# Output projection of a hybrid attention layer: six of eight pairs as three couples of seven block products each, with operands made beside attention and kept in DRAM

## The chip, the cores and the metric

The kernel runs on 1 core of one Trainium2 chip. The metric is the device time of one execution in microseconds (us). Before the change it is 680.48 us, the median of 3 runs (680.47 to 680.68).

The engines go by these names: PE multiplies matrices (PEld is its weight load), DVE, ACT and POOL work element by element, SP issues most of the DMA transfers. Each engine runs its own instructions strictly in order and waits on semaphores for what others make.

## The reference

One layer over 1024 rows of 1024 columns. After an adaptive layer norm, one input projection feeds 8 forgetting-attention heads and 8 stick-breaking heads of 64 columns each; their gated outputs go through one output projection, are scaled by a gate, added to the scaled input and normalised again.

```python
u = _layer_norm(x) * (1.0 + scale[:, None, :]) + shift[:, None, :]
h = u @ w_in[layer]
fq, fk, fv, fg, ff, sq, sk, sv, sg = _split_columns(h)
...
y_fox = _from_heads(jnp.concatenate(fox_out, axis=2)) * jax.nn.silu(fg)
y_sb = _from_heads(jnp.concatenate(sb_out, axis=2)) * jax.nn.silu(sg)
y = jnp.concatenate([y_fox, y_sb], axis=-1) @ w_out[layer]
resid = DEEPNORM_ALPHA * x + gate[:, None, :] * y
x = _layer_norm(resid, ln_g[layer], ln_b[layer])
```

## The kernel before, in words

**Precision.** A matrix operand is kept as two parts: a rounded one ("hi", in the type fp32r) and the remainder ("lo"). A product of two such operands takes three matmuls, hi x hi, lo x hi and hi x lo. Making the two parts costs an engine two operations: a rounding copy and a subtraction.

**Work units.** The 16 heads are taken as 8 pairs: pairs 0 to 3 stick-breaking, 4 to 7 forgetting attention. A unit (p, h, i) is one head h of pair p and one block i of 128 query rows, 128 units in all. In a unit PE makes the scores S (L483, L484). For a stick-breaking unit ACT takes sigmoids, DVE scans (L514, L518) and POOL makes the product `be` (L520); for a forgetting unit DVE, ACT and POOL (`a`, L499) make the softmax. Two units later (LAG = 2) PE transposes the result (T, L537) and multiplies it with the values (pv, L554); POOL applies the gate path (ty, L570), and the outcome goes to DRAM (`y_dr`, L578), pair 7's to SBUF as y7h, y7l.

**Order.** PE's order is written out by hand. Between the units stand small steps of "filler": the projections of the following pairs (m for q, k and gate, L312 to L314; v, L370 to L372), rationed by FILL per pair. The other engines' order comes from a scheduler that places instructions by its own estimate of times.

**Weights.** `fetch_w` brings a piece of projection weight: a DMA into a raw tile (L123, tag "wraw", only 2 buffers), the rounding copy (L127) and the remainder (L128) on POOL, into a ring of RING = 5. An m weight is fetched as two halves (named 3_1_0, 3_1_1 for pair 3, matrix 1), a v weight, which serves two pairs, as four quarters (v1_0 to v1_3).

**Output projection before.** During pairs 4 to 6 `gen_split_out` (L890 to L899) takes 16 pieces of w_out through the same fetch, with a gate product (L125) ahead, and stores both parts in `wo_dr`. `load_y` (L910 to L918) loads gated outputs again and splits them on POOL. `o_step` (L937 to L939) is the projection itself: 8 row blocks, 2 column halves (the last block in 512, 256 and 256 columns), 8 pairs, 3 matmuls each. It runs as `tail` beside the last units and behind them; `o_half` adds the residual, normalises and stores.

## Time and profile before

The times and the profile are of the kernel before. Spans and busy times are of one profiled execution.

| what | us |
| --- | --- |
| time, median of 3 runs | 680.48 |
| span of the profiled execution, first to last instruction | 678.6 |
| what lies around the span, by the difference to the median | 1.9 |
| PE busy | 668.3 |
| DVE busy | 485.9 |
| POOL busy | 405.2 |
| ACT busy | 382.6 |

No device time of the profiled execution is given apart from its span; its own time is taken as the span with the 1.9 us around it. A row of a group of instructions reads: line, engine, operation, output and inputs with their shapes, count, then busy time in us and the mean of one in ns, then the idle time of the engine just ahead of them and what ended it. A row of a timeline reads: start, duration, engine, line, operation. A row of a DMA issue ends with the KB of one and the median time from issue to landing. Matmuls overlap, so the durations of single ones add up to more than the time that passes.

### The profile page before, as it was taken

What the parts mean: (1) busy time and instruction counts of PE and PEld (TensorE: products, weight loads), DVE (VectorE), ACT (ScalarE), POOL (GpSimd) and SP (SyncE); (2) the same over time, 40 slices, a digit from 0 to 9 for tenths busy, and PEclk for the clock granted to TensorE, in tenths of its full rate; (3) what the DMA queues carried; (4) which work ended last, traced back from release to release, by engine and by line L of the source; (5) the groups of instructions that cost most, each with busy time, mean ns of one, the idle gap of its engine ahead of it and who ended that gap; (6) DMA issues with size and microseconds to landing.
All of it is one profiled execution on the core that took longest, in us unless ns stands there. A gap on an engine that the chain in (4) does not pass through costs nothing.

```text
span 678.6 us, 11231 instructions
## 1 busy us (share of the span) xinstructions
PE 668.3 (98%) x3713; PEld 571.2 (84%) x3713; DVE 485.9 (72%) x1001; ACT 382.6 (56%) x889; POOL 405.2 (60%) x530
## 2 busy tenths in 40 slices
PE   8999999999999999999999999999999999999995
PEld 4888898888998888889988888889988888888885
DVE  6787779868677777686776675766676777775645
ACT  5576468757567667576675564655565766521000
POOL 5560279755357556556378878785785365655412
PEclk9999999999999999999999999999999999999998
DMA  9983432112101112122124555263452297153301
GB/s 326 401 312 126 139 79 75 41 28 67 29 20 56 54 42 57 40 54 56 49 93 144 151 164 174 87 201 112 127 169 59 70 350 302 59 177 107 120 32 63
DMA packets 46474, 81.55 MB, mean 120 GB/s; under 512 B 5264, under 2 KB 20176, under 8 KB 46416
## 3 DMA queue, kind: packets, MB, share of 16 engines
q1 hardware_dynamic: 44832, 76.37, 35.1%
q10 hardware_dynamic: 1584, 4.47, 2.1%
q8 instruction: 29, 0.48, 0.3%
q14 instruction: 29, 0.24, 0.1%
HBM read 60.34 MB, written 16.29 MB: 113 GB/s over the span
## 4 chain that ended last, share of the span: by engine, by line
PE 97%; DMA 1%; DVE 0%; POOL 0%; ACT 0%; issue 0%; SPq 0%; POOLq 0%
PE m L312 11%; PE m L314 10%; PE m L313 10%; PE pv L554 10%; PE T L537 9%; PE S L484 5%; PE S L483 5%; PE o L939 4%; PE o L937 4%; PE o L938 4%; PE v L370 4%; PE v L372 4%; PE v L371 4%; PE st_q L647 1%; PE st_k L647 1%; PE st_late L647 1%
## 5 line engine op out<-in xcount | busy, mean ns | idle before, releaser
L540 DVE TENSOR_TENSOR pt<-T,pt 128x512 fp32r<-128x512 f32 (+2 forms) x192 | 102.7, 553 | 43.8 <-ACT pt L539 42.2
L539 ACT CAST pt<-T 128x512 fp32r<-128x512 f32 (+2 forms) x192 | 88.9, 479 | 64.5 <-PE T L537 62.5
L312 PE MATMUL m<-uh,whi 128*128 128x512 f32 x304 | 123.3, 405 | 0.1
L314 PE MATMUL m<-uh,wlo 128*128 128x512 f32 x304 | 119.8, 394 | 0.0
L313 PE MATMUL m<-ul,whi 128*128 128x512 f32 x304 | 119.7, 394 | 0.0
L520 POOL TENSOR_TENSOR be<-be,kp 128x127 f32<-128x127 f32 (+3 forms) x64 | 78.9, 1234 | 36.2 <-DVE kp L518 24.4
L554 PE MATMUL pv<-pt,v 128*128 128x512 f32 x320 | 82.8, 388 | 0.0
L514 DVE TENSOR_TENSOR_SCAN kp<-kp,floor 128x128 f32<-128x128 f32 (+3 forms) x64 | 58.6, 915 | 17.6 <-ACT kp L506 17.4
L499 POOL TENSOR_SCALAR a<-a,l 128x1024 f32<-128x1024 f32 (+3 forms) x64 | 48.4, 756 | 34.3 <-DVE l L497 26.0
L483 PE MATMUL S<-k,q 128*128 128x512 f32 (+5 forms) x192 | 68.8, 360 | 0.0
L314 PEld LDWEIGHTS m<-uh,wlo 128*128 128x128 f32 x304 | 57.1, 188 | 13.7
L496 ACT ACTIVATE a<-a,nm 128x1024 f32<-128x1024 f32 (+3 forms) x64 | 49.8, 779 | 28.6 <-DVE nm L491 28.1
L312 PEld LDWEIGHTS m<-uh,whi 128*128 128x128 f32 x304 | 57.2, 188 | 10.2 <-PE T L537 0.3
L484 PE MATMUL S<-kl,qz 128*128 128x512 f32 (+5 forms) x192 | 65.2, 341 | 0.0
L313 PEld LDWEIGHTS m<-ul,whi 128*128 128x128 f32 x304 | 57.3, 188 | 9.0
L554 PEld LDWEIGHTS pv<-pt,v 128*128 128x128 f32 x320 | 55.5, 189 | 8.9
L570 POOL TENSOR_TENSOR ty<-ty,sg 64x256 f32<-64x256 f32 x64 | 46.9, 733 | 23.4 <-issue 12.2
L491 DVE CUSTOM_DVE_ANT_0 a<-S,fb 128x1024 f32<-128x1024 f32 (+3 forms) x64 | 48.2, 753 | 16.9 <-PE S L484 12.0
L456 ACT CAST qz<-q 64x128 fp32r<-64x128 f32 x128 | 37.3, 296 | 34.2 <-PE S L484 33.0
L506 ACT ACTIVATE kp<-S 128x384 f32<-128x384 f32 (+4 forms) x96 | 44.0, 494 | 21.5 <-PE S L484 20.2
L370 PE MATMUL v<-whi_v,uh 128*128 128x256 f32 (+1 forms) x192 | 54.7, 285 | 0.0
L372 PE MATMUL v<-wlo_v,uh 128*128 128x256 f32 (+1 forms) x192 | 54.2, 282 | 0.0
(296 smaller groups left out, 1628.3 us busy)
## 6 DMA issues: line engine op xcount, KB each, us to landing
raw<-in_w_qkg_dram SPq DMA_DIRECT2D x38, 256.0 KB, 2.7
wss<-in_w_ss_dram SPq DMA_DIRECT2D x14, 512.0 KB, 8.1
x<-in_x_dram SPq DMA_DIRECT2D x8, 512.0 KB, 7.1
k<-k SPq DMA_DIRECT2D x32, 128.0 KB, 2.3
wg<-in_w_gate_dram SPq DMA_DIRECT2D x8, 512.0 KB, 4.9
raw_o<-in_w_out_dram SPq DMA_DIRECT2D x16, 256.0 KB, 3.0
fb<-f_dr ACTq DMA_DIRECT2D x8, 512.0 KB, 4.5
wo_dr<-whi_o SPq DMA_DIRECT2D x16, 256.0 KB, 2.1
```

The source lines that it names most:

```text
L312: nc.tensor.matmul(acc, hi[:, c], u_hi[kt][:, s], start=(kt == 0), stop=False)
L313: nc.tensor.matmul(acc, hi[:, c], u_lo[kt][:, s], start=False, stop=False)
L314: nc.tensor.matmul(acc, lo[:, c], u_hi[kt][:, s], start=False, stop=(kt == NB - 1))
L370: nc.tensor.matmul(acc[:, :n], u_hi[kt][:, ts_], hi[:, s], start=(kt == 0), stop=False)
L372: nc.tensor.matmul(acc[:, :n], u_hi[kt][:, ts_], lo[:, s], start=False, stop=(kt == NB - 1))
L483: nc.tensor.matmul(S[:, s, :w], qst[p][h][:, qs], kst[p][h][:, ks], start=True, stop=False)
L484: nc.tensor.matmul(S[:, s, :w], z, klo[p][:, ks], start=False, stop=True)
L520: nc.gpsimd.tensor_tensor(be[:, :ke - 1], be[:, :ke - 1], kp[:, 1:ke], op=ALU.mult)
L537: nc.tensor.transpose(tp[:, b * P:(b + 1) * P], a[:, kb * P:(kb + 1) * P], ident)
L539: nc.scalar.copy(hi[:, :n, qo:qo + P], t3)
L540: lows[:] = [nc.vector.tensor_tensor(lo[:, :n, qo:qo + P], t3, hi.bitcast(F32)[:, :n, qo:qo + P], op=ALU.subtract)]
L554: nc.tensor.matmul(acc2[:, :, q0:], vt[p][:, kb, h * P:(h + 1) * P], pt[:, :, q0:], start=(kb == 0), stop=(kb == last))
```

## The change

The output projection of pairs 0 to 5 is taken as three couples of two pairs (NC = 3). Row blocks are taken in four pairs (ROWS), columns in two halves, so each couple is a product of 2 x 2 blocks by 2 x 2 blocks. Instead of eight block products it makes seven from sums and differences of blocks (Winograd's form of Strassen's scheme): four early ones, A11 x B11, S2 x T2, S3 x T3, S1 x T1, and three late ones, P4, P2 and P3. Pairs 6 and 7 go the direct way (`plain`).

The operands are made in 28 pieces: `weight_piece` (12), `weight_plain` (4) and `y_piece` (12). Each loads into one of the two raw tiles, may multiply by the gate, is split by an ACT copy and a POOL subtraction (`halves`), then forms four sums of 128 columns in place (`less`: on POOL during pairs 1 to 3, on DVE later), is split again and stored to DRAM. `along` steps this beside the filler from pair 1 on, one step per PACE = 3 filler steps, so that a piece holds its raw tile for some 12 to 15 of them. Before, this work on w_out lay in pairs 4 to 6 alone. In the tail the loads read ready operands (`load_early`, `load_late`, `w_block`, `w_plain`), the accumulators are summed on ACT and DVE, and the residual is added by ACT and POOL half by half.

The core of the diff; the new tail follows these products in the order early 0, early 1, direct blocks, early 2, early 3, late ones, and the last row block by itself:

```diff
-    SPACE = 10
+    PACE = 3
...
+    NC = 3
+    ROWS = ((6, 7), (4, 5), (2, 3), (0, 1))
+    EARLY = (("A11", "B11"), ("S2", "T2"), ("S3", "T3"), ("S1", "T1"))
+    LATE = {"P4": ("A22", "T4"), "P2": ("A12", "B21"), "P3": ("S4", "B22")}
...
-            nc.gpsimd.tensor_tensor(be[:, :ke - 1], be[:, :ke - 1], kp[:, 1:ke], op=ALU.mult)
+            prods[:] = [nc.gpsimd.tensor_tensor(be[:, :ke - 1], be[:, :ke - 1], kp[:, 1:ke], op=ALU.mult)]
...
-    def gen_split_out():
-        for pr in range(NPAIR):
-            for h in range(2):
-                s = slice(h * 512, h * 512 + 512)
-                with after(*scaled[BEHIND:BEHIND + 1]):
-                    hi, lo = fetch_w(f"o{pr}_{h}", w_out[pr * P:(pr + 1) * P, s], 512, gate[:, s])
-                nc.sync.dma_start(wo_dr[0, pr, :, s], hi.bitcast(F32)[:, :512])
-                nc.sync.dma_start(wo_dr[1, pr, :, s], lo.bitcast(F32)[:, :512])
-                for _ in range(SPACE):
+    def tied():
+        return after(*(scaled[BEHIND:BEHIND + 1] or prods))
+
+    def halves(raw, n, key, to):
+
+        both = ring_set(key)
+        nc.scalar.copy(both[:, 0, :n], raw[:, :n])
+        with tied():
+            nc.gpsimd.tensor_tensor(both[:, 1, :n], raw[:, :n], both.bitcast(F32)[:, 0, :n], op=ALU.subtract)
+        return both.bitcast(F32)
+
+    def less(to, a, b, op=ALU.subtract):
+        eng = nc.vector if scaled else nc.gpsimd
+        with tied():
+            eng.tensor_tensor(to, a, b, op=op)
...
+    def weight_piece(c, q):
+        raw = raw_tile(f"ow_{c}_{q}")[:, :512]
+        r4 = raw.rearrange("p (a b q) -> p a b q", a=2, b=2)
+        cols = slice(q * P, q * P + P)
+        for a in range(2):
+            pr = 2 * c + a
+            nc.sync.dma_start(r4[:, a], w_out[pr * P:(pr + 1) * P, :].rearrange("p (b c) -> p b c", b=2)[:, :, cols])
+        yield
...
+        both = halves(raw, 3 * P, f"ob_{c}_{q}", None)
+        for x in range(2):
+            nc.sync.dma_start(wo_dr[c, 0:3, :, x, cols].rearrange("o p q -> p o q"),
+                              both[:, x, :3 * P].rearrange("p (o q) -> p o q", q=P))
+        yield
+        b21, b22, b11, b12 = parts_of(raw)
+        less(b11, b12, b11)
+        less(b12, b22, b12)
+        less(b22, b22, b11)
+        less(b21, b21, b22)
+        yield
+        both = halves(raw, 4 * P, f"ot_{c}_{q}", None)
...
+            _, make, *args = pieces.pop(at[0])
+            for _ in make(*args):
+                for _ in range(PACE):
                     yield
...
+    def block(t, late, what, acc, cols=slice(0, 512), ends=(True, True)):
+
+        y, w = what
+        for c in range(NC):
+            yh, yl = (y_set[t, c, late][:, x, Y_AT[y] * P:][:, :P] for x in range(2))
+            hi, lo = (v[:, cols] for v in wo[w, c])
+            nc.tensor.matmul(acc, yh, hi, start=(ends[0] and c == 0), stop=False)
+            nc.tensor.matmul(acc, yl, hi, start=False, stop=False)
+            nc.tensor.matmul(acc, yh, lo, start=False, stop=(ends[1] and c == NC - 1))
+            yield
...
+    def along(main, side):
+        for x_ in main:
+            next(side, None)
+            yield
...
-        gen_m(2, 0), gen_m(2, 1), gen_v(1),
-        beside(chain([gen_m(2, 2), gen_m(3, 0), gen_m(3, 1), gen_m(3, 2)]), gen_forget()),
-        gen_m(4, 0), gen_m(4, 1), gen_v(2),
-        beside(chain([gen_m(4, 2), gen_m(5, 0), gen_m(5, 1), gen_m(5, 2),
-                      gen_m(6, 0), gen_m(6, 1), gen_v(3), gen_m(6, 2),
-                      gen_m(7, 0), gen_m(7, 1)]), gen_split_out()),
+        along(chain([
+            gen_m(2, 0), gen_m(2, 1), gen_v(1),
...
+            gen_m(7, 0), gen_m(7, 1)]), operands),
```

How the instructions stand now is shown at three places. First, POOL around the first quarter of weight v1, which PE first uses behind the scores of unit (1,0,7) in both kernels. In before (whi and wlo are the two parts, be and kp a unit's product, ty a gated output):

```order
L127 TENSOR_SCALAR whi_2_1_1_1743<-raw_2_1_1_1741 128x512
L128 TENSOR_TENSOR wlo_2_1_1_1744<-raw_2_1_1_1741,whi_2_1_1_1743 128x512
L521 MEMSET be_0_1_5_1456 128x1
L520 TENSOR_TENSOR be_0_1_5_1456<-be_0_1_5_1456,kp_0_1_5_1455 128x767
L127 TENSOR_SCALAR whi_v1_0_1933<-raw_v1_0_1931 128x528
L128 TENSOR_TENSOR wlo_v1_0_1934<-raw_v1_0_1931,whi_v1_0_1933 128x528
L521 MEMSET be_0_1_6_1502 128x1
L520 TENSOR_TENSOR be_0_1_6_1502<-be_0_1_6_1502,kp_0_1_6_1501 128x895
```

In the changed kernel (w is a tile with both parts, ow a raw tile of w_out):

```order
L539 TENSOR_TENSOR be_1_0_6_1898<-be_1_0_6_1898,kp_1_0_6_1897 128x895
L955 TENSOR_TENSOR ow_0_2_1868<-ow_0_2_1868,gate_88 128x512
L146 TENSOR_SCALAR w_v1_0_1961<-raw_v1_0_1959 128x528
L589 TENSOR_TENSOR ty_1_0_1_1906<-ty_1_0_1_1906,sg_1_1279 64x256
L147 TENSOR_TENSOR w_v1_0_1961<-raw_v1_0_1959,w_v1_0_1961 128x528
L540 MEMSET be_1_0_7_1950 128x1
L539 TENSOR_TENSOR be_1_0_7_1950<-be_1_0_7_1950,kp_1_0_7_1949 128x1023
L146 TENSOR_SCALAR w_v1_1_1966<-raw_v1_1_1964 128x528
L147 TENSOR_TENSOR w_v1_1_1966<-raw_v1_1_1964,w_v1_1_1966 128x528
L146 TENSOR_SCALAR w_v1_2_1971<-raw_v1_2_1969 128x528
```

The first quarter's split moved from behind the product of unit (0,1,5) to behind that of (1,0,6), nine units later, and the second quarter's from behind (1,0,1) to behind (1,0,7).

Second, POOL around weight 3_1, which PE first uses behind the scores of unit (2,0,7). In before its first half stands around the product of (1,1,7):

```order
L127 TENSOR_SCALAR whi_3_1_0_2817<-raw_3_1_0_2815 128x512
L128 TENSOR_TENSOR wlo_3_0_1_2605<-raw_3_0_1_2602,whi_3_0_1_2604 128x512
L521 MEMSET be_1_1_7_2432 128x1
L520 TENSOR_TENSOR be_1_1_7_2432<-be_1_1_7_2432,kp_1_1_7_2431 128x1023
L128 TENSOR_TENSOR wlo_3_1_0_2818<-raw_3_1_0_2815,whi_3_1_0_2817 128x512
```

In the changed kernel (oy and w_ys are a piece of gated outputs):

```order
L934 TENSOR_TENSOR w_ys_0_0_2870<-oy_0_0_2718,w_ys_0_0_2870 128x512
L589 TENSOR_TENSOR ty_2_0_1_2860<-ty_2_0_1_2860,sg_2_2508 64x256
L540 MEMSET be_2_0_7_2912 128x1
L539 TENSOR_TENSOR be_2_0_7_2912<-be_2_0_7_2912,kp_2_0_7_2911 128x1023
L146 TENSOR_SCALAR w_3_1_0_2923<-raw_3_1_0_2921 128x512
L147 TENSOR_TENSOR w_3_1_0_2923<-raw_3_1_0_2921,w_3_1_0_2923 128x512
```

It moved eight units, to behind the product of the very unit behind whose scores PE uses it.

Third, POOL around weight 4_2, which PE first uses behind the scores of unit (4,0,7). In before:

```order
L520 TENSOR_TENSOR be_3_0_7_3541<-be_3_0_7_3541,kp_3_0_7_3540 128x1023
L127 TENSOR_SCALAR whi_4_2_0_4065<-raw_4_2_0_4063 128x512
L521 MEMSET be_3_1_0_3618 128x1
L128 TENSOR_TENSOR wlo_4_2_0_4066<-raw_4_2_0_4063,whi_4_2_0_4065 128x512
L520 TENSOR_TENSOR be_3_1_0_3618<-be_3_1_0_3618,kp_3_1_0_3617 128x127
```

In the changed kernel (a is a forgetting unit's softmax):

```order
L539 TENSOR_TENSOR be_3_1_7_4230<-be_3_1_7_4230,kp_3_1_7_4229 128x1023
L955 TENSOR_TENSOR ow_2_2_4261<-ow_2_2_4261,gate_88 128x512
L934 TENSOR_TENSOR w_ot_2_1_4203<-ow_2_1_4042,w_ot_2_1_4203 128x512
L518 TENSOR_SCALAR a_4_0_7_4289<-a_4_0_7_4289,l_4_0_7_4291 128x1024
L146 TENSOR_SCALAR w_4_2_0_4276<-raw_4_2_0_4274 128x512
L147 TENSOR_TENSOR w_4_2_0_4276<-raw_4_2_0_4274,w_4_2_0_4276 128x512
```

Its two parts moved from just behind the product of (3,0,7) to behind the softmax of (4,0,7), and on SP its load now follows the stores of the piece w_ot_2_1.

## The prediction

> **What bounds the kernel now.** I read the busy shares and the chain that ended last first, then PE's own waits, then busy time by stretch.

> ```profile
> PE 668.3 (98%) x3713; PEld 571.2 (84%) x3713; DVE 485.9 (72%) x1001; ACT 382.6 (56%) x889; POOL 405.2 (60%) x530
> PE 97%; DMA 1%; DVE 0%; POOL 0%; ACT 0%; issue 0%; SPq 0%; POOLq 0%
> PE sc_all L179 <- POOL ident masks.py:199: 1.5, 1, 1.5
> PE xT_early L256 <- ACT x L222: 0.9, 1, 0.9
> PE st_q L647 <- ACT uh L270: 0.4, 1, 0.4
> ```

> PE is busy for 98% of the span, and the whole list of what it waited for is these three, 2.8 us in the first 15. So any work taken off PE shortens the kernel by its own length, and any wait put in front of PE lengthens it by its own length: nothing stands by to absorb either.

> ```profile
> 136.80:341.00 204.20, 204.20 (x1215) 179.91 (x1215) 150.28 (x261) 134.66 (x326) 117.14 (x162) 1.00 0.18 47
> 640.00:660.00 20.00, 20.00 (x87) 16.15 (x87) 9.63 (x15) 0.00 (x0) 4.60 (x6) 1.00 0.14 53
> L937 PE MATMUL o<-woh,whi_y 128*128 128x512 f32 (+1 forms) x119 | 46.1, 388 | 0.0
> L937 PE MATMUL o<-woh,y7h 128*128 128x512 f32 (+1 forms) x17 | 6.5, 382 | 0.0
> ```

> The columns of a stretch are its length, then busy time and count of PE, weight load, DVE, ACT and POOL, then the granted clock. In 640 to 660 us, inside the output projection, 87 matmuls take 20.00 us: one 512-column matmul starts every 0.23 us. The 0.388 us of the group is each one's own duration, and they overlap, so removed matmuls are priced at 0.23. POOL is at 117 of 204 us in pairs 1 to 3 (136.8 to 341.0): the change lays new work on it there.

> **What is removed.** L937 to L939 have 119 + 17 each, 408 matmuls, worth 384 of 512 columns. In the new program seven block products for four row pairs, three couples and three matmuls are 252, and pairs 6 and 7 direct are 4 x 4 x 2 x 3 = 96: 348. So 36 x 0.232 = 8.4 us less for PE, all of it on the path.

> **What is added beside attention, and where it stands.** Every operand piece costs POOL an optional gate product, two remainders and four sums of 128 columns.

> ```profile
> L125 POOL TENSOR_TENSOR raw_o<-raw_o,gate 128x512 f32<-128x512 f32 x16 | 20.7, 1294 | 6.6 <-DMA raw_o<-in_w_out_dram 6.6
> L918 POOL TENSOR_TENSOR wlo_y<-yr,whi_y 128x384 fp32r<-128x384 f32 x8 | 8.1, 1018 | 0.5
> L520 POOL TENSOR_TENSOR be<-be,kp 128x127 f32<-128x127 f32 x8 | 3.7, 464 | 0.2 <-DVE kp L514 0.2
> L127 POOL TENSOR_SCALAR whi<-raw 128x512 fp32r<-128x512 f32 x38 | 23.5, 620 | 14.1 <-PE m L313 7.6 <-DMA raw<-in_w_qkg_dram 5.0 <-DVE l L497 0.6
> L128 POOL TENSOR_TENSOR wlo<-raw,whi 128x512 fp32r<-128x512 f32 x38 | 49.2, 1297 | 1.3 <-PE v L372 0.3
> L570 POOL TENSOR_TENSOR ty<-ty,sg 64x256 f32<-64x256 f32 x64 | 46.9, 733 | 23.4 <-issue 12.2 <-DVE ty L569 8.3 <-POOL a L499 0.8
> ```

> In pairs 1 to 3 the new program has 9 gate products, 14 remainders of 384 columns, 13 of 512 and some 52 sums: 9 x 1.29 + 14 x 1.02 + 13 x 1.30 + 52 x 0.46 = 67 us, so POOL goes from 117 to 184 of 204. The work itself still fits and costs nothing where POOL is idle; what costs is its place. A piece holds one of the two raw tiles for its whole life, so the fetches of the next pair's weights are left with one, and each half must be loaded, rounded and split before the next load may begin. In the new order they have slid back with it: in before the splits stand two to ten units ahead of PE's first use in pairs 1 to 3, mostly six or more, now zero or one (two for two halves).

> What such a place is worth is read from a unit's product, behind which the split now queues, and from a fetch:

> ```profile
> 162.18 1.33 POOL L128 TENSOR_TENSOR wlo_v<-raw_v,whi_v 128x528 fp32r<-128x528 f32 x1
> 167.05 0.28 PE L370 MATMUL v<-whi_v,uh 128*128 128x264 f32 x1
> 167.79 0.28 PE L370 MATMUL v<-whi_v,uh 128*128 128x264 f32 x1
> 237.94 0.39 PE L484 MATMUL S<-kl,qz 128*128 128x512 f32 x1
> 242.36 0.28 PE L484 MATMUL S<-kl,qz 128*128 128x128 f32 x1
> 242.85 2.00 POOL L520 TENSOR_TENSOR be<-be,kp 128x1023 f32<-128x1023 f32 x1 [1.52 <-DVE kp L518]
> 244.84 0.42 POOL L520 TENSOR_TENSOR be<-be,kp 128x127 f32<-128x127 f32 x1
> raw<-in_w_qkg_dram SPq DMA_DIRECT2D x38, 256.0 KB, 2.7
> raw_v<-in_w_vf_dram SPq DMA_DIRECT2D x4, 264.0 KB, 2.7
> ```

> From the last score matmul of a row block 7 (ends 238.33) to the end of its product on POOL (244.85) are 6.5 us; of a row block 0 (242.64 to 245.26) 2.6. A fetch is 2.7 + 0.62 + 1.30 = 4.6 us, 4.7 for the 528-column quarters. One quarter of a v weight gives PE 0.74 us of work (167.05 to 167.79) on first use; a half of another weight 12 x 0.232 = 2.8. In before even the last quarter of v1 was split (163.5) before PE began the first (167.05).

> Now the sites, in the order of the program. "After S" counts from the end of the scores behind which PE meets the weight.

> - **v1.** PE meets it right behind the scores of (1,0,7). The first remainder stands behind a y product of POOL that DVE feeds, some 4.3 us after S. The second quarter's load may start only then, and its split stands behind the product of (1,0,7), 6.5 after S: another 4.1. The third is a pure chain, 4.7 less 0.7: 4.0. The fourth has a unit of PE work ahead of it: 2.6. Sum 15.
> - **3_1.** The split stands right behind the product of (2,0,7), PE's use right behind its scores: 6.5 + 0.62 = 7.1 until the rounded half is there, and the remainder 1.30, of which two matmuls cover 0.46: 8.0.
> - **4_2.** The product of (3,1,7) ends 2.7 after the scores of (4,0,7), which is where PE wants the weight (3.8 us of PE work lie between the two scores). Behind it on POOL stand a gate product (1.29) and a remainder (1.30); SP has the store of that remainder queued ahead of the load, so load, rounding and remainder follow: 2.7 + 1.29 + 1.30 + 2.7 + 0.62 = 8.6, and 0.84 for the remainder: 9.5.
> - **v2 and v3**, like v1: v2's first remainder behind the product of (3,1,0) and four POOL operations (2.6 + 0.4 + 0.7 + 0.6 + 1.3 + 1.3 = 6.9), then 2.7, 1.2 and 0.8 of chain: 11.5. v3 by the same steps 10.5.
> - **2_2.** Second half's remainder behind the product of (1,1,7), with 2.8 of PE work since its scores: 6.5 + 1.3 - 2.8 = 5.0, and some more by queued sums: 5.3.
> - **2_1, 3_0, 3_2, 4_0, 4_1.** The chain between two halves, 4.6 plus an attention product of 0.4 to 2.0, against 2.8 of work: 1.8 to 3.8 each by that, 12.7 together with their places.

> Together 15 + 8.0 + 9.5 + 11.5 + 10.5 + 5.3 + 12.7 = 72.5 us. From 5_0 on the pieces are fewer and the splits two or more units ahead, v3 aside: nothing.

> The least that no idle POOL could remove is the fetch chain itself and the two products that stand ahead: v1 9, v2 5, v3 5, 3_1 7, 4_2 8, or 34 us. The most is not bounded by these rows: a split behind a piece is also a product behind a piece, and PE's transposes come two units (8.5 us at 204.2 / 48 per unit) after scores whose product takes 6.5, so 2 us of slack meet pieces of 1.0 to 1.3 an operation. I add nothing for that and up to 15 us for the range.

> **The clock.** After its last matmul PE is idle:

> ```profile
> 671.00:678.60 7.60, 0.46 (x4) 0.26 (x3) 3.58 (x8) 0.82 (x2) 1.84 (x4) 0.66 0.18 70
> 673.00:674.00 1.00, 0.00 (x0) 0.00 (x0) 1.00 (x3) 0.37 (x1) 0.55 (x1) 0.75 0.00 0
> 674.00:675.00 1.00, 0.00 (x0) 0.00 (x0) 1.00 (x3) 0.45 (x2) 0.82 (x2) 0.50 0.00 0
> ```

> The granted clock is at half some 2 us after work ended at 671.5. About ten of my waits are longer than that. How long the half clock would last into the work behind a wait no row shows: between nothing and a whole unit of 4.25 us at half speed, 2.1 us each, so 0 to 21. I take nothing in the sum, since several of these waits are followed by another at once, and keep 21 for the range. [...]

> **The tail.** Its loads are rows of 512 KB:

> ```profile
> wol<-wo_dr SPq DMA_DIRECT2D x8, 512.0 KB, 7.8
> ```

> The last early y operand of row pair 2 is loaded into a ring tile freed shortly before PE wants it, behind 1.5 MB on the same queue: a wait of 0 to 8, I take 3, in a stretch where POOL is at 4.6 of 20. Evacuations on DVE (9.6 of 20) and the end behind the last matmul, 7.1 us, stay as they are. ACT's rounding copies lie beside its 56%.

> **The sum.** On the profiled execution: 678.6 - 8.4 + 72.5 + 3 = 745.7. The median of the runs, 680.48, is 1.9 above the span, so 747.6, call it 748. Likeliest alone 725 to 770.

> **Rivals.**

> - *Only the bare chains wait.* POOL's real pace lets the splits through earlier than queued products of 6.5 us suggest (a stalled PE makes no new scores, so POOL catches up). Then 680.5 - 8.4 + 34 = 706. Against it: the order on POOL is fixed, and the 6.5 us run from PE's own last scores.
> - *Backlog and clock.* The transposes miss their products too, and half clock follows the waits: 748 + 15 to 36, 763 to 784. For it: POOL at 184 of 204.
> - *Faster.* Early waits push PE back against POOL and SP, the later splits regain their lead, and only the saving is left, 680.5 - 8.4 = 672. It decides at the point where the split's end lies before PE's first use, so the 6.5 us from score to product would have to shrink under 2. Nothing in the rows does.
> - *It does less than it says.* The matmuls go, but a wait of the same size comes, within 0.2% (1.4 us) of before, which is about what a measurement of this kernel can tell from no change. It needs all sites but one to vanish.

> **Chances.** Forecast 0.60, bare chains 0.13, backlog and clock 0.20, faster 0.05, no change 0.01, slower by less than 700 0.01. The range reaches from just under the bare chains, 705, into the third case, 785. Slower by over 0.2% is 0.94, within 0.01, faster 0.05.

> **What would show it.** PE's waits list, three rows before, should be led by m and v matmuls waiting for POOL's splits, v1 near 15 us and the sum near 70; PE's busy time should fall by 8 us at a full clock; POOL should be near 90% in pairs 1 to 3; the granted clock should dip behind the longest waits. I am wrong if those waits are under 30 us in sum, if the longest waits are for T on POOL's products, or if the time lost lies in the tail.

## The result, and the profile after

| what | before | after |
| --- | --- | --- |
| time, median of 4 runs each, us | 680.48 (680.26 to 680.68) | 783.12 (781.92 to 784.33) |
| ratio to before, 95% interval | | 1.1509 (1.1493 to 1.1525) |
| span of the profiled execution, us | 678.6 | 780.6 |
| matmuls | 3713 | 3668 |
| PE busy, us | 668.3 | 694.7 |
| mean granted clock of PE | 0.996 | 0.949 |

The kernel became 102.6 us slower, where 67.5 was forecast: inside the range, at its upper end. The page of the changed kernel, first its busy times, then PE and its granted clock in 40 slices, then the chain that ended last:

```profile
PE 694.7 (89%) x3668; PEld 577.8 (74%) x3668; DVE 507.9 (65%) x1050; ACT 428.2 (55%) x976; POOL 467.4 (60%) x605
PE   8999999876978879886996899995999999998895
PEclk9999999995989979998897999997899999999998
PE 11%; POOL 4%; DMA 3%; DVE 3%; ACT 2%; issue 1%; SPq 0%; POOLq 0%; DVEq 0%; ACTq 0%
```

Two things are to be read from the first line. PE stands idle for 780.6 - 694.7 = 85.9 us instead of 678.6 - 668.3 = 10.3, which is 75.6 more. And PE is busy for 26.4 us longer although it has fewer matmuls: the same work went slower. The slices say where: from the eighth on, in pairs 1 to 5, PE falls again and again to between 5 and 8 tenths, and the granted clock dips in several of the same places (the 10th, 12th, 15th, 19th, 22nd and 28th slice). The chain has PE at 11% where it had 97%: it no longer runs along PE.

What PE waited for (total, times, longest); before, this list had three rows and 2.8 us:

```profile
PE v L389 <- POOL w_v L146: 19.4, 8, 4.2
PE m L331 <- POOL w L146: 19.0, 4, 8.7
PE m L333 <- POOL w L147: 8.5, 6, 3.8
PE v L391 <- POOL w_v L147: 7.2, 9, 2.0
PE m L333 <- POOL be L540: 3.7, 5, 1.2
PE T L556 <- DVE pt L559: 3.4, 4, 2.6
PE o L1058 <- DMA w_ye<-yb_dr: 3.0, 1, 3.0
PE o_P L1058 <- DMA yl_att<-yb_dr: 2.3, 1, 2.3
```

L146 is the rounding copy and L147 the remainder of a projection weight on POOL, L331 to L333 and L389 to L391 the matmuls that use them. The first four rows are 54.1 us. Three smaller rows that name the zeroing L540, which on POOL stands right ahead of the product a split is queued behind, belong to the same waits: 61.0 in all, called split waits below. The transposes T, for which the forecast feared a backlog, wait 3.4.

The stretches around the sites of the forecast (columns as before: length, busy time of PE, weight load, DVE, ACT, POOL, then granted clock, DMA share, GB/s):

```profile
136.20:406.90 270.70, 227.21 (x1234) 190.84 (x1233) 152.45 (x262) 150.74 (x355) 186.38 (x257) 0.92 0.34 96
145.00:165.00 20.00, 15.69 (x75) 12.22 (x74) 11.11 (x18) 10.83 (x25) 14.90 (x23) 1.00 0.33 93
165.00:195.00 30.00, 20.26 (x93) 16.59 (x92) 12.58 (x22) 10.93 (x25) 19.54 (x24) 0.72 0.37 93
222.00:236.00 14.00, 9.14 (x38) 6.84 (x37) 7.72 (x13) 6.37 (x14) 11.07 (x14) 0.79 0.29 85
262.00:290.00 28.00, 20.91 (x96) 16.46 (x95) 13.70 (x21) 12.93 (x30) 15.85 (x22) 0.82 0.21 64
355.00:385.00 30.00, 21.19 (x123) 18.66 (x120) 12.88 (x24) 12.40 (x31) 20.98 (x28) 0.83 0.40 112
404.00:430.00 26.00, 17.17 (x87) 14.13 (x86) 12.08 (x28) 11.40 (x23) 15.27 (x18) 0.80 0.34 103
525.00:555.00 30.00, 20.45 (x106) 17.44 (x105) 10.74 (x30) 10.22 (x26) 16.84 (x18) 0.77 0.41 121
```

Length less PE's busy time is the idle time of a site. Beside it stands what the half clock cost there, worked out from the distances between matmul starts in the stretches of half clock against those of the same shapes in before:

| site (stretch) | idle forecast, us | idle measured, us | lost to half clock, us |
| --- | --- | --- | --- |
| v1 (165 to 195) | 15 | 9.7 | 4.1 |
| 2_2 (222 to 236) | 5.3 | 4.9 | 2.0 |
| 3_1 (262 to 290) | 8.0 | 7.1 | 2.9 |
| v2 (355 to 385) | 11.5 | 8.8 | 2.6 |
| 4_2 (404 to 430) | 9.5 | 8.8 | 1.9 |
| v3 (525 to 555) | 10.5 | 9.6 | 2.8 |
| 2_1 (145 to 165), 3_0, 3_2, 4_0, 4_1 together | 12.7 | 13.0 | 0 |
| tail | 3 | 7.2 | 3.2 |
| smaller waits elsewhere | 0 | 6 | 0 |

Pairs 1 to 3 take 270.7 us where they took 206.4 (the row shown later with the last experiment). POOL is busy for 186.4 of them, 184 was forecast, but that is 69% of the longer stretch and not 90%.

One site in full, 3_1. First PE (start, duration, instruction, the wait ahead of it), then POOL:

```profile
270.70 0.40 PE L503 MATMUL S<-kl,qz 128*128 128x512 f32 x1
278.01 0.79 PE L331 MATMUL m<-uh,w 128*128 128x512 f32 x1 [6.91 <-POOL w L146]
280.38 0.63 PE L332 MATMUL m<-ul,w 128*128 128x512 f32 x1
280.81 0.63 PE L333 MATMUL m<-uh,w 128*128 128x512 f32 x1
...
286.02 0.39 PE L332 MATMUL m<-ul,w 128*128 128x512 f32 x1
286.25 0.39 PE L333 MATMUL m<-uh,w 128*128 128x512 f32 x1
```

```profile
271.20 1.27 POOL L934 TENSOR_TENSOR w_ys<-oy,w_ys 128x512 fp32r<-128x512 f32 x1
...
275.37 2.00 POOL L539 TENSOR_TENSOR be<-be,kp 128x1023 f32<-128x1023 f32 x1 [1.67 <-DVE kp L537]
277.34 0.62 POOL L146 TENSOR_SCALAR w<-raw 128x512 fp32r<-128x512 f32 x1
278.04 1.28 POOL L147 TENSOR_TENSOR w<-raw,w 128x512 fp32r<-128x512 f32 x1
```

PE ends its scores at 271.10 and has nothing to do until the product of that very unit and the rounding copy behind it are through: 6.91 us, where the forecast had 7.1. Then its matmuls start 0.43 us apart (280.38 to 280.81) and only from 284.6 on 0.23 apart (286.02 to 286.25). That second loss is the clock:

```profile
274.00:274.50 0.50, 0.00 (x0) 0.00 (x0) 0.49 (x1) 0.13 (x1) 0.00 (x0) 0.88 1.04 389
274.50:275.00 0.50, 0.00 (x0) 0.00 (x0) 0.50 (x1) 0.00 (x0) 0.00 (x0) 0.50 1.06 336
278.00:284.50 6.50, 6.35 (x16) 4.66 (x17) 0.27 (x1) 0.59 (x1) 1.80 (x2) 0.50 0.19 43
284.50:284.90 0.40, 0.40 (x3) 0.27 (x3) 0.40 (x1) 0.00 (x0) 0.32 (x2) 0.85 0.00 0
```

It went to half at about 274.4, 3.3 us after the last matmul, and was back at 284.6, 6.6 us into the new work.

**The sum of after.** PE is idle for 75.6 us more. Of the 26.4 us of busy time, the matmuls taken away are -8.4, and the rest, 34.8, is slower work in three parts:

- 19.5 from half clock, the sum of the last column. In before the clock is not at half while PE works, from 4.5 us on.
- 10.9 from lost overlap. The last matmul ahead of a wait is counted with its own 0.40 us, where in a row of them one starts every 0.23; 51 waits of over 0.1 us at some 0.2 each make 10.
- Some 4.2 from starts a little further apart at full clock, spread over the whole kernel. What makes these is not known.

The half clock can be seen in the means too: a mean of 0.949 is 2 x 0.051 x 780.6 = 80 us at half. PE was busy for 44.5 of them, and half of that, 22, is what it would lose at half speed.

### The profile page after: what moved, and what is told of

Same layout as the page of the kernel before. It is cut to its first block, busy times and chain, and to the rows that moved or that the text cites. A ratio compares the mean times of both kernels' runs of the same rounds, so it can differ in the third digit from the quotient of the medians.

```text
span 780.6 us, 11574 instructions
## 1 busy us (share of the span) xinstructions
PE 694.7 (89%) x3668; PEld 577.8 (74%) x3668; DVE 507.9 (65%) x1050; ACT 428.2 (55%) x976; POOL 467.4 (60%) x605
## 3 DMA queue, kind: packets, MB, share of 16 engines
q1 hardware_dynamic: 85088, 106.79, 42.4%
## 5 line engine op out<-in xcount | busy, mean ns | idle before, releaser
L331 PE MATMUL m<-uh,w 128*128 128x512 f32 x304 | 125.1, 412 | 23.0 <-POOL w L146 19.0
L333 PE MATMUL m<-uh,w 128*128 128x512 f32 x304 | 122.4, 403 | 12.6 <-POOL w L147 8.5
L332 PE MATMUL m<-ul,w 128*128 128x512 f32 x304 | 120.6, 397 | 0.0
L573 PE MATMUL pv<-pt,v 128*128 128x512 f32 x320 | 86.8, 403 | 0.0
L331 PEld LDWEIGHTS m<-uh,w 128*128 128x128 f32 x304 | 57.6, 190 | 36.1 <-POOL w L146 21.8
L333 PEld LDWEIGHTS m<-uh,w 128*128 128x128 f32 x304 | 57.7, 190 | 32.0 <-POOL w L147 12.9
L518 POOL TENSOR_SCALAR a<-a,l 128x1024 f32<-128x1024 f32 (+3 forms) x64 | 48.0, 749 | 50.8 <-DVE l L516 36.6
L389 PE MATMUL v<-w_v,uh 128*128 128x256 f32 (+1 forms) x192 | 58.3, 304 | 19.4 <-POOL w_v L146 19.4
L573 PEld LDWEIGHTS pv<-pt,v 128*128 128x128 f32 x320 | 58.5, 199 | 10.2 <-DVE pt L559 0.4
L391 PE MATMUL v<-w_v,uh 128*128 128x256 f32 (+1 forms) x192 | 58.2, 303 | 8.7 <-POOL w_v L147 7.2
L332 PEld LDWEIGHTS m<-ul,w 128*128 128x128 f32 x304 | 57.8, 190 | 8.6
L390 PE MATMUL v<-w_v,ul 128*128 128x256 f32 (+1 forms) x192 | 56.4, 294 | 0.0
L389 PEld LDWEIGHTS v<-w_v,uh 128*128 128x128 f32 x192 | 38.5, 200 | 22.0 <-POOL w_v L146 21.7
## 6 DMA issues: line engine op xcount, KB each, us to landing
raw<-in_w_qkg_dram SPq DMA_DIRECT2D x38, 256.0 KB, 3.0
wss<-in_w_ss_dram SPq DMA_DIRECT2D x14, 512.0 KB, 8.2
wo_dr<-w_ot SPq DMA_DIRECT2D x24, 256.0 KB, 2.4
ys_dr<-w_ys SPq DMA_DIRECT2D x12, 512.0 KB, 3.3
x<-in_x_dram SPq DMA_DIRECT2D x8, 512.0 KB, 6.8
```

The lines of the kernel that those rows point to most:

```text
L331: nc.tensor.matmul(acc, hi[:, c], u_hi[kt][:, s], start=(kt == 0), stop=False)
L332: nc.tensor.matmul(acc, hi[:, c], u_lo[kt][:, s], start=False, stop=False)
L333: nc.tensor.matmul(acc, lo[:, c], u_hi[kt][:, s], start=False, stop=(kt == NB - 1))
L389: nc.tensor.matmul(acc[:, :n], u_hi[kt][:, ts_], hi[:, s], start=(kt == 0), stop=False)
L391: nc.tensor.matmul(acc[:, :n], u_hi[kt][:, ts_], lo[:, s], start=False, stop=(kt == NB - 1))
L573: nc.tensor.matmul(acc2[:, :, q0:], vt[p][:, kb, h * P:(h + 1) * P], pt[:, :, q0:], start=(kb == 0), stop=(kb == last))
```

## The experiments

The theory of the forecast is one of *place*: the split of a projection weight stands too late in POOL's order, so PE reaches the weight first. Its rivals: *capacity* (POOL simply has too much to do), *the raw tile* (the pieces hold one of two), *the tail* (the new projection itself costs the time) and, for what the waits don't explain, *the clock*. The split waits of the runs, beside the times:

| kernel | time, us | ratio (95%) | split waits, us | units from split to first use, median |
| --- | --- | --- | --- | --- |
| after | 783.12 | 1.1509 (1.1493 to 1.1525) | 61.0 | 0 to 3, 1 |
| less_dve | 779.43 | 1.1456 (1.1422 to 1.1489) | 56.6 | 0 to 3, 1 |
| own_ty | 754.86 | 1.1097 (1.1068 to 1.1125) | 28.8 | 0 to 4, 2 |
| ahead6 | 740.36 | 1.0881 (1.0850 to 1.0913) | 24.9 | 0 to 10, 2 |
| ahead_ty | 749.81 | 1.1020 (1.0984 to 1.1057) | 0 | 2 to 11, 4.5 |
| apart | 703.70 | 1.0336 (1.0313 to 1.0358) | 3.9 | 2 to 11, 6 |
| hold_only | 702.98 | 1.0334 (1.0313 to 1.0355) | 0 | 2 to 9, 5 |

The last column is counted in the traces over the weights 2_1 to 4_2, v1 and v2: the units whose scores PE has begun when it first uses a piece of weight, less the units whose product POOL had begun ahead of its split. Before has 2 to 11, median 7.

### Only the tail: tail_only and tail_only2

Each piece is reduced to its stores, from a tile of the layer's input:

```diff
-        both = halves(raw, 3 * P, f"yb_{c}_{t}", None)
-        nc.sync.dma_start(yb_dr[t, c], both[:, :, :3 * P])
+        for x in range(2):
+            nc.sync.dma_start(yb_dr[t, c][:, x], u_hi[x].bitcast(F32)[:, :3 * P])
```

> The changed kernel with its operand pieces reduced to their stores: no loads, gate products, roundings, remainders or sums; what is stored is a tile of the layer's input, so the output projection multiplies wrong numbers. The new tail and the DMA stores stay. If what costs is the pieces beside attention (both the raw tile theory and the full POOL theory): PE's waits for weight splits vanish, only the tail's waits of some 7 us stay, and the time is 680.5 - 8.4 + 7 to 11, so 679 to 684. If the tail itself or the stores carry a large part: over 700.

Measured: 735.09 us, ratio 1.0811 (1.0794 to 1.0828). It missed 679 to 684, but as a total this tells nothing, since the stores, which now waited for no piece, all went out at the start and held up its loads: pair 1's first scores come at 184.7 us instead of 136.4. From there on it can be read. The lengths of the pairs, from first scores to first scores, are those of before to 0.1 us in pairs 1 to 5 (72.0, 67.2, 67.2, 72.6, 69.8), and from pair 7's first scores to PE's last matmul it is 128.7 us against 124.8. So the tail with 8.4 us less to multiply takes 3.9 us more, with nothing beside it in the earlier pairs.

The second try ties each store behind a product of attention:

```diff
+            with tied():
+                nc.sync.dma_start(wn_dr[n, :, x, s], u_hi[x].bitcast(F32)[:, :512])
```

> The changed kernel whose pieces are only their stores (of a tile of the layer's input, so the projection's operands are wrong), each store now held back behind a product of its unit as the pieces' POOL work is, since in the first form all 27 MB of stores went ahead of the start's loads. The new tail, no piece work beside attention. Expected: no waits beside attention, the tail's 7 us, 680.5 - 8.4 + 7 to 11 = 679 to 684. If stores and the new tail cost more than that: over 690.

Measured: 733.99 us, ratio 1.0788 (1.0755 to 1.0820). The tie did not hold the stores back, and they went out at the start again: inconclusive in the same way (by the rows of the first try its stores are 24 MB, not 27). From pair 7's first scores to the last matmul it takes 127.8 us.

### The raw tile: hold_only and own_ty

In hold_only a piece takes its raw tile, keeps it for as many filler steps and stores two ACT copies; the sums, remainders and gate products are gone:

```diff
-            nc.gpsimd.tensor_tensor(both[:, 1, :n], raw[:, :n], both.bitcast(F32)[:, 0, :n], op=ALU.subtract)
+            nc.scalar.copy(both[:, 1, :n], raw[:, :n])
...
-        with tied():
-            eng.tensor_tensor(to, a, b, op=op)
+        pass
```

> The changed kernel whose pieces still load and hold a raw tile for their 12 to 15 filler steps, but do nothing on POOL or DVE: both parts are ACT copies, the gate product and the sums are left out, so the projection's operands are wrong. Raw tile theory (a piece holds one of two raw tiles, so fetches come late): waits for splits stay near 60 us and the time is over 755. Full POOL theory (the pieces' POOL work delays the splits, the held tile hardly matters): those waits fall under 10 us, the granted clock stays near 1, and the time is 682 to 695.

Measured: 702.98 us, ratio 1.0334 (1.0313 to 1.0355), and no split wait at all. The longest rows of PE's list:

```profile
PE T L556 <- DVE pt L559: 4.9, 8, 1.2
PE S L502 <- ACT be L527: 3.4, 3, 1.9
```

The waits are as the second theory has them; the time lies 8 us above its 682 to 695. In the program a piece keeps its raw tile for as many steps as in after, but the trace shows that it is not held for as long: from the issue of a piece's load to the last read of the tile it is 14.0 us in the median of the 28 pieces, where after has 23.8. So a piece's load and its steps do not by themselves delay a split. What a tile held for as long as in after would do without the pieces' work on POOL is not shown. The kernel is still 22.5 us slower than before, with the waits spread over transposes, scores and the tail.

In own_ty the pieces get tiles of another pool, the two of the gated outputs ("ty"), and both raw tiles are the fetches' again:

```diff
+    def piece_tile(name):
+        return sb.tile([P, 512], F32, tag="ty", bufs=2, name=name)
...
-        raw = raw_tile(f"oy_{c}_{t}")[:, :512]
+        raw = piece_tile(f"oy_{c}_{t}")[:, :512]
```

> The changed kernel with the pieces' raw tiles taken from the two ty tiles in place of the two raw tiles of the weight fetches; all the work stays. Raw tile theory: the fetches have both raw tiles again, waits for splits fall under 15 us, time under 715. Full POOL theory: POOL carries the same work, the splits come at most a unit or two earlier, waits of 25 to 60 us stay, time 720 to 775. Against both, gated outputs could wait for a ty tile: then new waits for pv.

Measured: 754.86 us, ratio 1.1097 (1.1068 to 1.1125).

```profile
PE v L392 <- POOL w_v L149: 13.7, 3, 5.7
PE o L1061 <- DMA w_ye<-yb_dr: 10.0, 4, 5.6
PE v L394 <- POOL w_v L150: 7.2, 4, 4.0
```

About half of the split waits went (61.0 to 28.8), so the shared tile had a part in them, and half stayed with two raw tiles free for fetches. Time and waits lie in the ranges of the theory that POOL's work delays the splits. PE now waits 10.0 for the tail's early loads (3.0 in after), so some of the gain was given back there.

### Capacity: less_dve

The sums go to DVE from the start, which takes 24 us off POOL (467.4 to 443.6):

```diff
-        eng = nc.vector if scaled else nc.gpsimd
+        eng = nc.vector
```

> The changed kernel with the pieces' four sums on DVE in pairs 1 to 3 as well, in place of POOL: some 24 us of POOL's 184 of 204 go, but the weight splits keep their places in POOL's order, zero or one unit ahead of PE's use. Capacity theory (POOL is too full to reach the splits in time): waits fall by a third or more, 740 to 765. Place theory (a split is late because it is placed late, however idle POOL is): same waits, 775 to 788.

Measured: 779.43 us, ratio 1.1456 (1.1422 to 1.1489); split waits 56.6. POOL 24 us lighter gives 3.7 us back. The splits stand as far ahead as in after, 0 to 3 units, and the time is the one that the place theory expected.

### Place: ahead6 and ahead_ty

In ahead6 the fetch of the next weight is written 6 filler steps into the work on the present one, and not at its end; nothing else is touched:

```diff
+            for step, _ in enumerate(g):
+                if step == at and n + 1 < len(gens):
+                    next(gens[n + 1])
+                    primed = True
+                yield
...
-        along(chain([
+        along(chain_ahead([
...
+            gen_m(7, 0), gen_m(7, 1)], 6), operands),
```

> The changed kernel with the fetch of each projection weight written some ten filler steps earlier in the program (beside the seventh step of the weight before); pieces, raw tiles and POOL's work are as in the changed kernel. In the order the splits then stand one to six units ahead in pairs 1 to 4 except v2 and parts of v1 and 3_0. Place theory: waits fall to 20 to 35 us, 715 to 745. Capacity theory: the waits for splits stay over 50, over 765.

Measured: 740.36 us, ratio 1.0881 (1.0850 to 1.0913), 42.8 us better than after with the same work on POOL (465.9).

```profile
PE v L389 <- POOL w_v L146: 9.2, 6, 3.8
PE m L331 <- POOL w L146: 8.0, 2, 4.1
```

Ahead_ty is both edits, ahead6 and own_ty.

> Both at once: fetches written earlier as in the run before, and the pieces' raw tiles taken from the ty tiles, so that fetches have both raw tiles. POOL's work is unchanged. In the order all splits but one stand two to ten units ahead. Place theory: waits for splits under 5 us, clock near 0.99, the tail's 7 to 10 us of waits stay, 690 to 705. Capacity theory: over 740.

Measured: 749.81 us, ratio 1.1020 (1.0984 to 1.1057): the expected 690 to 705 was missed.

```profile
PE pv L576 <- DVE ty L591: 28.9, 4, 9.5
PE o L1061 <- DMA w_ye<-yb_dr: 8.6, 3, 5.4
```

Not one split wait is left, but 28.9 us came back at another name. The pieces hold the two tiles that a unit's outputs need, so a value product (pv) waits until the outputs before it have left its accumulator. The wait moved with the tile.

### The clock: warm, b_wait and b_wait_busy

Warm is after with extra matmuls at four of the sites, into the accumulator that the site's own product then overwrites, so that PE is not idle there:

```diff
+    KEEP = {(3, 1): 30, (4, 2): 37, 1: 11, 2: 18}
...
+            nc.tensor.matmul(acc, u_hi[0][:, :P], u_hi[1][:, :512], start=True, stop=True)
```

> The changed kernel with dummy matmuls on ready data in PE's order ahead of the four longest waits: 30 ahead of weight 3_1 (7.0 us), 37 ahead of 4_2 (8.6 us), 11 ahead of v1 and 18 ahead of v2. PE is busy instead of idle there. Clock theory (a wait of over some 3.5 us halves the clock for up to 7 us after work is back): the half clock behind 3_1 and 4_2 is gone, 3.0 + 1.9 us, and part of that behind v1 and v2 (4.4 + 2.7), so 774 to 779 us. Waits-alone theory (PE waits for POOL in any case, the slow matmuls only fill later waits): 782 to 786.

The 3.5 and 7 us of the clock theory are to be held against after: its four waits of over 3.5 us (3.84, 4.22, 6.91 and 8.68) all have the clock at half within them or 0.9 us behind them, and at 3_1 it stays so for 6.6 us of work.

Measured: 786.26 us, ratio 1.1541 (1.1499 to 1.1583); expected was 774 to 779, so it missed. At the places where the matmuls were put the half clock went (loss behind 3_1 from 2.9 us to none, behind 4_2 from 1.9 to none), but it appeared at others. The stretches 145 to 165, which nothing was put into, and 262 to 290:

```profile
145.00:165.00 20.00, 16.77 (x67) 12.89 (x66) 9.45 (x15) 9.44 (x22) 14.30 (x21) 0.83 0.32 91
262.00:290.00 28.00, 27.23 (x137) 22.02 (x135) 16.09 (x24) 15.31 (x36) 17.17 (x25) 1.00 0.26 82
```

In after the clock was 1.00 in the first and 0.82 in the second; here it is 0.83 and 1.00. The first has the same instructions in both kernels. Whether waits of 2 to 3 us halve the clock is thus not settled by the waits' length alone. The loss from half clock over the whole kernel was 22.6 us against 19.5, so this run could not price it.

The price was then taken in the kernel before, where nothing else waits. In b_wait five first-half splits, and nothing else, are held behind the product of their unit:

```diff
+    HOLD = ("2_1_0", "3_0_0", "3_1_0", "4_0_0", "4_1_0")
...
-        nc.gpsimd.tensor_scalar(hi[:, :n], raw, 1.0, 1.0, op0=ALU.mult, op1=ALU.mult)
+        with after(*(prods if key in HOLD else ())):
+            nc.gpsimd.tensor_scalar(hi[:, :n], raw, 1.0, 1.0, op0=ALU.mult, op1=ALU.mult)
```

> The kernel before, with no operand pieces at all; only five weight splits (2_1, 3_0, 3_1, 4_0, 4_1, first halves) are held back behind the product of the unit behind whose scores PE uses them. Place theory: each costs the time from scores to product plus 0.62 and 0.84, less PE's work between: 4.7, 4.7, 8.0, 6.6 and 5.3, or 29 us, and some 2 for lost overlap: 711 without a clock effect. Clock theory: besides, matmuls behind each wait run at half speed for some microseconds, 2 to 3 each: 718 to 726. If the splits' place were not the cause of PE's waits: 681.

Measured: 723.14 us, ratio 1.0638 (1.0620 to 1.0655).

```profile
PE m L315 <- POOL whi L130: 24.2, 5, 7.2
PE m L317 <- POOL wlo L131: 3.9, 5, 1.5
```

The waits are 28.1 us where 29 was expected, and the kernel is 42.9 slower, inside the range of the clock theory. In the profiled execution, which is 41.9 longer than that of before, half clock costs 11.3 beside the waits and lost overlap some 3: 28.1 + 11.3 + 3 = 42.4. No piece, no new tail and no busier POOL is in this kernel: a late split alone does what after shows, and costs half as much again as the wait. B_wait_busy puts matmuls into the same five waits:

```diff
+    KEEP = {(2, 1): 16, (3, 0): 16, (3, 1): 30, (4, 0): 24, (4, 1): 19}
```

> The run before with PE kept busy through most of each wait by dummy matmuls on ready data (16, 16, 30, 24 and 19 of 0.232 us, 24 of the 29 us). Clock theory: nothing behind the waits runs slowly, the granted clock is back at 0.996, and the time is 708 to 713, some 8 to 14 below the run without dummies. If the half clock costs nothing that matters: the same time as that run, or longer by up to 3.

Measured: 713.87 us, ratio 1.0496 (1.0480 to 1.0512); the mean granted clock goes from 0.975 to 0.998.

```profile
core 0: 720.5 us, clock 0.975
```

```profile
core 0: 711.6 us, clock 0.998
```

With the weight still as late, 9.3 us of 42.9 are gone, and the time is 0.9 above the expected 708 to 713. That is what the half clock cost over five waits, 1.9 each; by the matmul starts its loss goes from 11.3 us to none, 2.3 each.

### Fetches and pieces apart: w22_all and apart

Both let pieces advance only in stretches of the filler in which no fetch is open, and write fetches early; all of the pieces' work stays on its engines and in the raw tiles. Both also mend the tail's waits with tiles that are free by then and with one normalisation for both halves. W22_all loads one operand over ACT's DMA queue:

```diff
+            at, low, stages = (22, 1, 10) if n in (2, 9, 16) else (2, 4, 6)
...
+                if step == at and n + 1 < len(gens):
+                    next(gens[n + 1])
+                    primed = True
...
+                if step >= low and (step - low) % 2 == 0 and budget[0] > 0:
+                    next(side, None)
+                    budget[0] -= 1
...
-                load_late(c, 0, att_tile("yl_att", F32R) if c == 2 else None)
+                load_late(c, 0, att_tile("yl_att", F32R) if c == 2 else None, nc.scalar if c == 2 else None)
```

> An attempt at a better version of the change: each fetch is written at the third step of the weight before (for the weight behind a v at its 23rd), and the pieces are stepped only in windows behind that, so that a piece's raw tile and a fetch's don't meet; in the tail one early operand gets a tile of its own, one late operand goes over ACT's DMA queue, and the second half's normalisation goes to ACT and POOL. All but the splits of 2_2 and 4_2 (zero to two units ahead) stand three to ten units ahead. Place theory: some 10 us for 2_2 and 4_2 with their clock, 5 to 13 for other waits as in the run with held raw tiles, the tail 0 to 5 over before less 0 to 5 mended: 690 to 705. Capacity theory: over 730. Faster than before only if the tail's mending brings more than the two weights lose, which I don't expect.

Measured: 725.13 us, ratio 1.0663 (1.0643 to 1.0683); missed its 690 to 705.

```profile
PE o L1067 <- issue: 12.8, 1, 12.8
PE m L333 <- POOL w L147: 7.4, 2, 4.4
PE o_P L1067 <- DMA yl_att<-yb_dr: 7.0, 1, 7.0
```

The pieces were now too slow: the last ones were not done when PE wanted the tail's first operand (12.8). The wait for the load that was moved to ACT's queue is 7.0, where after has 2.3. Pairs 1 to 3 took 219.0 us (after 270.7).

Apart gives the pieces denser stretches from weight 4_2 on, and loads the operand that was late first, into a tile of the finished keys:

```diff
+            at, low, stages, stride = (12, 1, 5, 2) if n in (2, 9, 16) else (2, 4, 10, 1) if n > 10 else (2, 4, 6, 2)
...
-            for c in range(NC):
-                load_late(c, 0, att_tile("yl_att", F32R) if c == 2 else None)
+            for c in (2, 0, 1):
+                load_late(c, 0, big("kl", 2, "yl_kl", F32R) if c == 2 else None)
```

> The changed kernel with its pieces and fetches kept apart, all of its work unchanged: a fetch is written at the third step of the weight before (behind a v at its thirteenth), the pieces are stepped only in windows behind that (one piece beside a weight up to 4_2, two beside each later one), so that all are done before the tail's first load; in the tail one early operand has a tile of its own, one late operand lies in the last free key tile and is loaded first, and the second half's normalisation goes to ACT and POOL. In the order the splits stand two to ten units ahead (v3's last two one), as in the kernel before. Place theory: waits for splits under 3 us, clock above 0.99, 5 to 10 of other waits beside attention and in the tail against the 8.4 saved: 677 to 689. Capacity theory (POOL's 67 us more in pairs 1 to 4): over 720. Faster than before only below 679.

Measured: 703.70 us (5 runs), ratio 1.0336 (1.0313 to 1.0358); it missed 677 to 689.

```profile
PE T L556 <- DVE pt L559: 4.9, 7, 1.4
PE S L502 <- DVE nm L510: 4.3, 4, 2.5
PE v L391 <- POOL w_v L147: 1.9, 2, 1.1
```

The split waits are 3.9 us in all. Pairs 1 to 3 in before, and then in apart:

```profile
136.40:342.80 206.40, 206.40 (x1234) 182.11 (x1233) 152.38 (x262) 136.31 (x328) 118.85 (x165) 1.00 0.18 47
```

```profile
136.20:345.40 209.20, 207.70 (x1235) 182.22 (x1234) 152.97 (x262) 146.15 (x348) 165.85 (x232) 1.00 0.37 104
```

POOL is at 165.85 of 209.20 us, 79%, more than the 69% of after, and PE stands still for 1.5 us only, at full clock. Here capacity falls as the cause of the split waits: POOL is fuller than in after, and the splits are in time. Over the whole kernel POOL does as much as in after (467.1 against 467.4 us), but not all of it in the same place: in pairs 1 to 3 it is 165.9 us where after has 186.4, so some 20 us have moved behind them. That the forecast's whole load fits into pairs 1 to 3 is therefore not shown.

Where apart still loses its 24.4 us of span against before, by pairs: 2.8 in 1 to 3, 4.5 + 9.9 + 6.5 in 4, 5 and 6, then -2.4 from pair 7's first scores to the last matmul, and 3.3 behind it (10.4 against 7.1). In pairs 4 to 6 PE waits for evacuated transposes (pt) and for the softmax's maxima (nm), both on DVE, where the pieces' sums and ACT copies stand among the units' own. That these cause the waits is argued from the names; no run took them away alone. No version was faster than the kernel before.

## Why the prediction was right in its sign and short in its size

**Matmuls removed, -8.4: right, and worth nothing in the end.** The terms of the busy time close with it: -8.4 + 19.5 + 10.9 + 4.2 = 26.2 of 26.4. But the new tail gives it back within itself. From pair 7's first scores to the end of the span after takes 134.9 us against 131.9: -8.4, 7.2 of waits, 3.2 of half clock, 1.0 of overlap. Tail_only shows the same without anything beside attention.

**Waits, 72.5 + 3: right, the sum partly by luck.** Measured 75.6 (76.2 behind the first 16 us). The sites were the right ones, and the m weights came within a microsecond. The three v weights came out 5.3, 2.7 and 0.9 shorter than worked out. At v1 the first remainder was ready 4.3 us after the scores, as forecast; but the quarters cost 3.8, 2.9, 2.9 and 0.2 us where 4.3, 4.1, 4.0 and 2.6 were forecast. PE's work ahead of the fourth took 5.2 us at half clock and hid its chain. The tail was forecast 4 too short, and 6 us in smaller waits for DVE and for splits elsewhere were not foreseen. That these errors cancel to within 0.2 us is luck.

**"I take nothing in the sum": the step that failed.** The clock was given 0 out of 0 to 21; it cost 19.5. The reason for the zero was that "several of these waits are followed by another at once", which shortens no half-clock stretch: the row of 3_1 has the clock at half for 6.6 us into the work, and at v1 the clock stayed low across the quarters (0.72 over 30 us). The upper end for one wait, 2.1 us, was too low as well: 3_1 lost 2.9, v3 2.8, and v1 with its several waits 4.1. Only because eight places were hit and not ten waits does the whole stay under 21. From 175.4 us on every change of the clock in after lies on one grid of 3.41 us (more under the last heading), and how long the half clock lasts into the work does not follow the length of the wait: 6.6 us at 3_1 behind a wait of 6.91, 4.5 us at 4_2 (416.7 to 421.2) behind one of 8.68.

**Lost overlap: a term that was not there.** A wait of length w costs w and about 0.2 us more, because the matmuls ahead of it and behind it no longer overlap: 10.9 over 51 waits. The rows for it stood in the prediction itself, 0.388 us for one matmul and 0.23 from one to the next. With the 4.2 us of wider starts at full clock, for which there was no term either, 19.5 + 10.9 + 4.2 = 34.6 is nearly all of the 35.1 us by which the forecast fell short.

**The cause of the waits: half right.** That place decides and not the amount of work holds: less_dve (24 us less on POOL) gives 3.7, ahead6 (same work, earlier fetches) gives 42.8, apart (same work, fetches and pieces apart) 79.4, of which some 2 are its mended tail, and b_wait makes the same kind of loss out of nothing but late splits. But the held raw tile was named as what moves the splits, and in hold_only, where a piece keeps it for as many steps, no split waits. There it is held for 14.0 us and not 23.8, since no POOL operation, tied behind a product, must run before it comes free. So it seems to take a held tile *and* the piece's POOL operations; this is argued. Own_ty and ahead6 each remove somewhat over half of the split waits. How much the tile and the operations have by themselves is not told apart further.

**The rivals.** "Only the bare chains wait" (706) fell as a time: its five sites, priced at 34 us, waited 44.0, and there were 32 more elsewhere. But v1 (9.7 against 9) and 3_1 (7.1 against 7) were near its prices, not near the full ones. "Backlog and clock" (763 to 784) holds the time only by chance: its backlog did not come, the transposes waiting 3.4 us, its clock alone gives 748 + 19.5 = 767, and the other 15 us are lost overlap and wider starts, which it did not name. "Faster" (672) fell twice: the leads did not come back, and even apart, in which they do, is at 703.7.

## What to carry to other kernels

In a kernel whose main engine hardly waits (here PE was busy for 98% of the span), side work is not free because another engine has room for it: in less_dve 24 us less on POOL gave 3.7 us, and in b_wait five late splits alone cost 42.9. What counts is behind which instruction of that engine's queue the next operand of the main engine ends up, and that can be read from the order before a run. An estimate from these runs for a wait in front of such a PE is its length, 0.2 us for lost overlap (10.9 us over 51 waits in after), and some 2 to 3 us of half clock where it is long: by after at 3_1, 4_2 and 2_2, with some 4 to 9 us of waiting (2.9, 1.9 and 2.0 us lost), and by b_wait, where five waits cost about 2 each. Where two kinds of work shared the raw tiles, moving one of them to another pool of two tiles, with early fetches, moved the wait (ahead_ty: no split wait, 28.9 us at pv); writing the fetch earlier and the side work into the gaps between fetches took the split waits from 61.0 to 3.9 us (apart).
